# The second mixer's 24 feature chunks as pairs of seven block products, and its attention steps behind 14 gate chunks

## The chip, the core and the metric

The kernel runs on one core of a Trainium2 chip. The metric is the device time of one execution, in microseconds (us). Before the change three executions took 2940.22, 2941.33 and 2941.63 us, with a median of 2941.33 us. The profile was taken in an execution of its own.

## What is computed

The reference is one layer of a hybrid decoder on 512 prompt tokens and 8 sample tokens (N = 520 columns, kept as two halves of 260), all in float32. Cut to what matters here:

```python
sh1, sc1, g1, sh2, sc2, g2 = ada_mod(c, w_ada, b_ada)
h = modulate(rmsnorm(x, norm1_w), sh1, sc1)
mq, mk, mv, mo, mi, mf, fq, fk, fv, ff, ga, gb = jnp.split(h @ w_in + b_in, SPLIT_POINTS, axis=-1)
...                                       # the mLSTM mixer makes y_m
q_f = rmsnorm(split_heads(fq, F_HEADS), f_qnorm_w)
k_f = rmsnorm(split_heads(fk, F_HEADS), f_knorm_w)
y_f = fox_fn(q_f, k_f, v_f, lf_f)         # prompt: causal; sample: over pages of a cache
merged = jax.nn.sigmoid(ga) * (y_m @ w_proj_a) + jax.nn.sigmoid(gb) * (y_f @ w_proj_b)
x = x + g1 * (merged @ w_out)
...                                       # a gated feed-forward layer with a causal convolution
```

`h @ w_in` is the product that the change touches. Its columns are taken in chunks of 128 features: 1 chunk of forget and input gates, 24 of the mLSTM mixer, 24 of the second mixer (`fq`, `fk`, `fv` of 8 heads), 16 of `ga` and 16 of `gb`.

## The kernel before

**Two forms of the product.** A chunk of 128 features needs the 2048 inputs in 16 blocks of 128, times 520 columns. Every float32 operand is split into a high and a low part (`wh`, `wl` for weights, `hh`, `hl` for `h`), and three products of parts make one. `dense` (L206) does a chunk as it stands: 16 blocks, 3 products, 2 halves, 96 matmuls of 128x260, so 192 for two chunks. `Pair` (L255) does two chunks together as a 2 by 2 block product with seven block products instead of eight: 7 products of 8 blocks and 3 parts, 168 matmuls of 128x260. For it VectorE adds pieces of the raw weights (`total`, tiles `sw`), ScalarE and VectorE split seven blocks of weights, and the results in three accumulators `x`, `y` and `z` are put together by short additions (tiles `tt`, `tg`). `run_pairs` (L336) writes its instructions in a fixed order.

**Where the work around them stands.** `dense` calls `step` after each of the 16 blocks, and `step` takes the next entry of the list `bg`: a piece of an attention, or `None`. It also calls `due`, which now and then takes a step of `pending`, one of the 16 steps by which a slice of the `w_ada` product is made (two loads of 512 KB and four groups of matmuls, tile `adp`). A scheduler then orders the instructions of each engine, except inside `run_pairs`.

The stages that matter, with their times in the profile (from the span's start):

- 292 to 461 us, the mLSTM heads: dense chunks, with the mLSTM attention in `bg`.
- 461 to 574 us: `w_proj_a` (`pa`), dense, with `pending` making slice G1. Two dense gate chunks go before it (`NG` = 2).
- 574 to 736 us: 16 gate chunks (14 of `ga`, 2 of `gb`) in 8 units of `GatePair`. The forms of `h` that the seven products need (`hX`) are made during `pa`.
- 736 to 1084 us: the 24 chunks `fi` of the second mixer, dense, 3 for each head; slice SC2 in `pending`; the attention of a head in `bg` behind its chunks.
- 1084 to 1281 us: the other 14 chunks of `gb` (`gate`), dense; slice SH2 in `pending`; the attention of the sample tokens over the cache's pages in `bg`.
- 1281 to 1376 us: `w_proj_b` (`pb`), dense, and the merge.

**A head's attention** (L1141 to L1218): squares of q and k (`sq`, split into `hi` and `lo`; GpSimd makes `lo`), their sums by TensorE (`ms`), an inverse root by `rsqrt`, the split of q and k (`fqh`, `fql`, `fkh`, `fkl`; GpSimd makes the low parts), the spread of the forget row (`nFb`, copied to `nfb`), four blocks of scores (`fS`) with softmax (tiles `fs`, `sm`), their transposes (`fPT`), and the product with the values (`fy`).

**The sample's attention** (L1251 to L1336): GpSimd gathers 32 pieces of key pages (`kp`) and 32 of value pages (`vp`) by indirect DMAs. VectorE multiplies each `kp` with a broadcast query (`qb`) and sums it into `sc` (`s_scores`, kept in program order). A softmax follows (`sS`), its transposes (`sPT`), a memset of `pp` by GpSimd, and TensorE's products `sO` with `vp`, each four followed by a copy `ob` and transposes `sOT`.

Of the kernel before, what the change touches and what calls it, by code (L numbers as in the profile page):

```python
# [38 lines left out]
FQ, FK = 4, 7  # L39
FW = (2, 0, 0, 0, 4, 0)  # L40
# [25 lines left out]
def tile_hybrid_step(ctx: ExitStack, tc: tile.TileContext, I, O):  # L66
# [294 lines left out]
    def rsqrt(parts, scale, out=None):  # L361

        v, r, t = pt("rv"), out or st("rr"), pt("rt")
        for ps, a, b in parts:
            S.activation(r[:, a:b], ps, AF.Ln, scale=scale, bias=eps)
            V.tensor_scalar(v[:, a:b], ps, scale, EPS, op0=ALU.mult, op1=ALU.add)
# [599 lines left out]

    for hh in range(MH):
        H = Head()
        H.i, H.vt, H.hm, H.v, H.o = hh, [], [], [], []
        H.q = m_proj("q")  # L970
        H.k = m_proj("k")
        bg += [None, on(m_decay, H), on(m_rows, H), None, None, None]
        bg += [on(m_scores, H, j) for j in range(NB)] + [on(m_dots, H)]
        H.v = [m_proj("v"), m_proj("v")]
        bg += [None, on(m_values, H, 0), on(m_values, H, 1), on(m_states, H), None, on(m_den, H), None, on(m_bound, H),
               on(m_keys, H), None, None, None, on(m_num, H, 0), None, on(m_num, H, 1), None, on(m_state, H)]
        H.o = [m_proj("o"), m_proj("o")]
        bg += [None] * 12 + [on(m_tokens, H)] + [None] * 6 + [on(m_out, H)]
# [4 lines left out]
    def w_gate(j, which):  # L983
        i = 1 + 24 + 24 + which * KC + j
        acc = dense(I["w_in"][i], h, "gate")
        sg = st("sgm")
        S.activation(z2(sg), acc, AF.Sigmoid, bias=col(C_BIN + i - 1))
        return sg

    pending += ada_steps(G1)  # L990
    calls[1:] = 9, 10
# [29 lines left out]
    dsg = dram([NG, P, N], "dsg")  # L1021

    class GatePair(Pair):
        def __init__(self, gates, order):
            self.gates = gates
            super().__init__([I["w_in"][49 + g] for g in gates], hX, order, 1)
# [13 lines left out]
        def out(self, e):  # L1040

            g = self.gates[e]
            parts = (self.tt[:, :HN], self.tg[:, :HN]) if e == 0 else (self.tg[:, HN:N], self.tt[:, HN:N])
            for z, t in enumerate(parts):
                o = slice(z * HN, (z + 1) * HN)
                if g < KC:
                    V.tensor_tensor(t, t, self.pa[e][:, o], op=ALU.mult)
                G.dma_start((dmg[g] if g < KC else dsg[g - KC])[:, o], t)

        def after(self, r):  # L1050
            if r > 10:
                return
            b = [col(C_BIN + 48 + g) for g in self.gates]
            if r == 7:
                S.activation(self.tg[:, HN:N], self.x, AF.Sigmoid, bias=b[1], scale=-1.0)
                self.pa = []
                for g in self.gates:
                    self.pa.append(pt("pao") if g < KC else None)
                    if g < KC:
                        nc.sync.dma_start(self.pa[-1][:, :N], dmg[g])  # L1060
            if r == 8:
                S.activation(self.tt[:, HN:N], self.tt[:, HN:N], AF.Sigmoid, bias=b[1], scale=-1.0)
                S.activation(self.tt[:, :HN], self.tt[:, :HN], AF.Sigmoid, bias=b[0])
                S.activation(self.tg[:, :HN], self.tg[:, :HN], AF.Sigmoid, bias=b[0])
# [6 lines left out]
    gates = list(range(NG, KC + NG))  # L1071
    units = [GatePair(gates[2 * i:2 * i + 2], ORDER if i else ORDER1) for i in range(KC // 2)]
# [66 lines left out]
    yf = []  # L1139

    def f_norm(t, w, out):  # L1141
        r = rsqrt(sums_r(out.sq), 1.0 / DK)
        V.scalar_tensor_tensor(t[:, :N], t[:, :N], w, r[:, :N], op0=ALU.mult, op1=ALU.mult)

    def f_norm_k(H):
        f_norm(H.k, col(C_KN), H)
        G.dma_start(O["kT"][:, H.i, :], H.k[:, :N])
        V.tensor_copy(kS[:, :, H.i], H.k[:, SEQ:N])
        H.kr = split(sp, "s", H.k, "fk", SEQ, G)

    def f_norm_q(H):
        if H.i == 0:
            log_exp()
        f_norm(H.q, qwc, H)
        V.tensor_copy(qS[:, :, H.i], H.q[:, SEQ:N])
        H.qr = split(sp, "s", H.q, "fq", SEQ, G)

    def f_square(H, t):
        sq = pt("sq")
        S.activation(sq[:, :N], t[:, :N], AF.Square)  # L1160
        H.sq = parts_r(sq)

    def f_values(H):

        ps = mm_ps("vtp")
# [11 lines left out]
    def f_scores(H, i):  # L1177
# [13 lines left out]
        V.tensor_scalar(s[:, :n], s[:, :n], sm[:, 1:2], None, op0=ALU.mult)  # L1191
# [16 lines left out]
    def f_attend(H, j):  # L1208
# [8 lines left out]
        yf.append(split(sp, "s", H.y, "yf", SEQ))  # L1217
        H.vt = H.last = H.y = None  # L1218

    def f_proj(H, i):  # L1220
        acc, t, n = w_in("fi")
        S.activation(z2(t), acc, AF.Identity, bias=col(C_BIN + n - 1))
        return t

    pending += ada_steps(SC2)
    calls[:] = 0, 1, 3
    for hh in range(FH):
        H = Head()
        H.i, H.p, H.pt = hh, [], []
        H.q = f_proj(H, 0)  # L1230
        f_square(H, H.q)
        bg += [None] * FQ + [on(f_norm_q, H)]
        H.k = f_proj(H, 1)
        f_square(H, H.k)
        bg += [None] * FK + [on(f_norm_k, H)]
        H.v = f_proj(H, 2)
        G.dma_start(O["vT"][:, hh, :], H.v[:, :N])
        V.tensor_copy(vS[:, :, hh], H.v[:, SEQ:N])
        bg += [None] * FW[0] + [on(f_forget, H)] + [None] * FW[1] + [on(f_values, H)] + [None] * FW[2]
        for i in range(NB):  # L1240
            bg += [on(f_scores, H, i)] + [None] * FW[3]
        bg += [None] * FW[4] + [on(f_turn, H, j) for j in range(NB)] + [None] * FW[5]
        bg += [on(f_attend, H, j) for j in range(NB)]
# [7 lines left out]
    def s_rows():  # L1251
        ps = mm_ps("qSt")
        T.transpose(ps[:64, :P], qS.rearrange("p b h -> p (b h)"), ident)
        qrow = pt("qrow")
# [3 lines left out]
    def s_load(i):  # L1258

        b, e = divmod(i, 2)  # L1260
        qb = pt("qb")
        nc.sync.dma_start(qb[:, :512], dqf[b, e * 512:(e + 1) * 512].partition_broadcast(P))
        W.k[i] = [qb]
        for g in range(NPG):
            kp = pt("kp")
# [15 lines left out]
    def s_softmax():  # L1281
        pqk = pt("pqk")[:, :64]
# [25 lines left out]
    def s_gather(i):  # L1308

        e, g, b = i // 8 % 2, i // 4 % 2, i // 16 * 4 + i % 4  # L1310
        W.v[i] = pt("vp")
        gather(W.v[i][:, :512], I["cache_v"], idx_h[e][:, b * NPG + g:b * NPG + g + 1])

    def s_attend(n):
# [7 lines left out]
        if g == 1:  # L1322
            W.ob = pt("ob")
# [14 lines left out]
    bg += [s_rows] + [None] * 12 + [on(s_load, 0), None, None, on(s_load, 1)] + [None] * 5  # L1338
    for i in range(NS * 2):
        bg += [on(s_scores, i), None] + ([on(s_load, i + 2)] if i + 2 < NS * 2 else []) + [None] * 2  # L1340
    bg += [s_bias, None, s_softmax] + [None] * 6 + [s_weights] + [None] * 4
    bg += [on(s_gather, i) for i in range(6)] + [None] * 4
    for n in range(8):
        bg += [on(s_attend, n)] + [on(s_gather, i) for i in range(n * 4 + 6, min(n * 4 + 10, 32))]
        bg += [on(s_heads, n // 2)] if n % 2 else [None]
        bg += [None] * 3
    mg = []
    for j in range(KC):
        if j == 0:
            assert not pending  # L1350
            pending += ada_steps(SH2)
            calls[:] = 0, 1, 2
        if j < NG:
            mg.append(st("sgm"))
            nc.sync.dma_start(mg[j][:, :N], dsg[j])
        else:
            mg.append(w_gate(j, 1))
# [147 lines left out]
    early = {}  # L1505
    for n, j in enumerate(order):
# [15 lines left out]
        if n == KC - 1:  # L1522
            units[0].load((1, 0), (1, 1))
        old = pt("mgo")
# [624 lines left out]
```

## Time and profile before

| what | value |
|---|---|
| median of the runs | 2941.33 us |
| the profiled execution | 2941.65 us |
| its span, first to last instruction | 2940.0 us |
| TensorE's granted clock, mean | 0.997 |
| HBM read, written | 436.64 MB, 62.73 MB |
| stage of the 24 `fi` chunks | 348 us |
| stage of the 14 `gate` chunks | 197 us |

The span and the execution's own time differ by 1.65 us, which lie around the span. Busy times are sums by engine; "PE" is TensorE's matmuls, "PEld" its weight loads, DVE is VectorE, ACT ScalarE, POOL GpSimd, SP the engine that issues most loads. TensorE's matmuls are pipelined, so a matmul's duration (283 ns for 128x260) is longer than its distance to the next; the distance is read from a count of matmuls in a stretch without idle time.

### The profile page before, as it was taken

To read this page: it belongs to the slowest core of one execution; us is meant where nothing else is said; L and a number is where in the kernel's file an instruction comes from. 1 tells how busy PE (TensorE), PEld (TensorE's weight loads), DVE (VectorE), ACT (ScalarE), POOL (GpSimd) and SP (SyncE) were. 2 spreads that over 40 slices of the span, in tenths; PEclk is the share of its full clock that TensorE was granted. 3 is DMA by queue.
4 is the path that set the end of the run, shared out by engine and by line. 5 is a ranking of instruction groups with operands and counts; after the bars stand their busy time and mean duration, and the time that the engine had idled before them with its cause. 6 is when DMAs were issued, how large, how long until landed. Compare 5 with 4: busy or idle time off the path is not lost. (4 is left out here: it accounts for less than half of the span.)

```text
span 2940.0 us, 58499 instructions
## 1 busy us (share of the span) xinstructions
PE 2883.5 (98%) x23627; PEld 2750.5 (94%) x23627; DVE 2129.8 (72%) x3866; ACT 1292.4 (44%) x2182; POOL 424.1 (14%) x662
## 2 busy tenths in 40 slices
PE   6999999999999999999999999999999999999999
PEld 4888998899999999899999999999999999999999
DVE  4777875578455556248888888888888887788787
ACT  4234433355444442234555444444444455544543
POOL 0003431201111114411211100000000001100100
PEclk9999999999999999999999999999999999999999
DMA  9833437945444348767673343444444436745843
GB/s 339 285 108 112 146 123 261 293 146 166 137 133 143 120 165 298 256 207 223 199 239 111 101 151 126 147 140 149 133 138 140 144 122 183 190 155 190 205 159 109
DMA packets 209592, 506.67 MB, mean 172 GB/s; under 512 B 22624, under 2 KB 75216, under 8 KB 209320
## 3 DMA queue, kind: packets, MB, share of 16 engines
q1 hardware_dynamic: 174000, 412.24, 42.9%
q0 software_dynamic: 34880, 90.45, 10.2%
q8 instruction: 185, 3.03, 0.4%
q14 instruction: 87, 0.71, 0.1%
q10 hardware_dynamic: 440, 0.23, 0.0%
HBM read 436.64 MB, written 62.73 MB: 170 GB/s over the span
## 5 line engine op out<-in xcount | busy, mean ns | idle before, releaser
L62 PE MATMUL x<-bf,wh 128*128 128x260 f32 x2624 | 476.8, 283 | 1.0 <-DVE tg L62 0.5
L62 ACT CAST wh<-sw 128x512 fp32r<-128x512 f32 x584 | 334.9, 621 | 244.4 <-PE z L62 86.9
L62 DVE TENSOR_TENSOR wl<-sw,wh 128x512 fp32r<-128x512 f32 x584 | 375.9, 685 | 69.7 <-ACT wh L62 66.8
L62 PEld LDWEIGHTS x<-bf,wh 128*128 128x128 f32 x2624 | 403.6, 188 | 1.4 <-DVE tg L62 0.7
L180 DVE TENSOR_TENSOR wl<-raw,wh 128x1024 fp32r<-128x1024 f32 (+1 forms) x168 | 208.6, 1243 | 265.9 <-ACT wh L179 249.9
L62 DVE TENSOR_TENSOR wl<-raw,wh 128x1024 fp32r<-128x1024 f32 (+2 forms) x283 | 310.6, 1105 | 118.5 <-ACT wh L62 114.5
L62 ACT CAST wh<-raw 128x1024 fp32r<-128x1024 f32 (+2 forms) x283 | 268.1, 956 | 234.3 <-PE x L62 128.9
L62 PE MATMUL x<-bf,wl 128*128 128x260 f32 x1312 | 369.6, 282 | 0.0
L179 ACT CAST wh<-raw 128x1024 fp32r<-128x1024 f32 (+1 forms) x168 | 173.4, 1033 | 354.3 <-PE gate L222 68.5
L62 PEld LDWEIGHTS x<-bf,wl 128*128 128x128 f32 x1312 | 247.0, 188 | 0.0
L62 PE MATMUL y<-bf,wh 128*128 128x260 f32 x1312 | 240.6, 284 | 2.9 <-ACT wh L62 2.4
L62 PEld LDWEIGHTS y<-bf,wh 128*128 128x128 f32 x1312 | 202.7, 189 | 3.4 <-ACT wh L62 2.6
L62 PE MATMUL x<-ff,wh 128*128 128x260 f32 x1024 | 186.3, 282 | 0.0
L62 PE MATMUL y<-bf,wl 128*128 128x260 f32 x656 | 185.8, 283 | 0.2 <-DVE wl L62 0.2
L62 DVE TENSOR_TENSOR sw<-raw,raw 128x512 f32<-128x512 f32 x288 | 185.0, 683 | 0.4 <-DMA tot<-sq 0.4
L222 PE MATMUL fi<-hh,wh 128*128 128x260 f32 x768 | 162.3, 293 | 0.0
L62 PEld LDWEIGHTS x<-ff,wh 128*128 128x128 f32 x1024 | 157.9, 188 | 0.0
L222 PE MATMUL fi<-hl,wh 128*128 128x260 f32 x768 | 155.0, 283 | 0.0
L222 PE MATMUL fi<-hh,wl 128*128 128x260 f32 x768 | 154.1, 282 | 0.0
L62 PE MATMUL x<-ff,wl 128*128 128x260 f32 x512 | 144.7, 283 | 0.0
L222 PEld LDWEIGHTS fi<-hh,wh 128*128 128x128 f32 x768 | 118.5, 189 | 15.9 <-ACT wh L179 6.7
L62 PE MATMUL fo<-fe,wh 128*128 128x260 f32 x768 | 125.7, 284 | 1.9 <-DVE fo L62 1.1
(585 smaller groups left out, 7448.6 us busy)
## 6 DMA issues: line engine op xcount, KB each, us to landing
raw<-in_w_fi SPq DMA_DIRECT2D x176, 512.0 KB, 4.5
raw<-in_w_in SPq DMA_DIRECT2D x156, 512.0 KB, 4.8
ar<-in_w_ada SPq DMA_DIRECT2D x192, 256.0 KB, 6.0
raw<-in_w_ada SPq DMA_DIRECT2D x96, 512.0 KB, 4.0
raw<-in_w_fo SPq DMA_DIRECT2D x64, 512.0 KB, 4.1
raw<-in_w_out SPq DMA_DIRECT2D x32, 512.0 KB, 4.7
raw<-in_w_fo SPq DMA_DIRECT2D x32, 384.0 KB, 4.3
dff<-cc POOLq DMA_DIRECT2D x44, 260.0 KB, 4.0
```

The lines of the kernel that those rows point to most:

```text
L62: return lambda *a, **k: self.tc.keep_in_program_order(getattr(self.eng, op)(*a, **k))
L179: S.copy(wh[:, o], t[:, :m])
L180: V.tensor_tensor(wl[:, o], t[:, :m], wh[:, o].bitcast(F32), op=ALU.subtract)
L222: T.matmul(acc[:, z, :HN], a[:, o], b[:, z * HN:(z + 1) * HN], start=(k == 0 and i == 0), stop=(k == K - 1 and i == 2))
```

## The change

The 24 chunks `fi` leave the dense form and join the gate chunks in `MixPair`: 12 units for the second mixer ahead of the 8 units of gates, 20 units in one run. A unit's features are written to a DRAM tensor `dfi` and read back by `f_load`, a head at a time. The 24 dense chunks behind which the attention stood are gone, so all of the second mixer's attention, the prompt's and the sample's, stands behind the 14 dense `gate` chunks, in 14 x 16 = 224 slots, by a table of times (`plan`, `at`).

Three sets of steps move: slice G1 of `w_ada` goes from the `pa` stage to the mLSTM heads, SC2 from the `fi` stage to the two gate chunks and `pa`, and SH2 stays. In the attention, the scaling of the softmax and one of `rsqrt`'s two first steps go from VectorE to ScalarE. The sample's tiles move to the larger pool. The output of heads 0 to 3 is written to DRAM (`dyf`) and read back late (`f_again`). The dense gate chunks are stored without the sigmoid (`dsg`), read back in the `pb` stage (`mg_load`), and the sigmoid is taken there.

```diff
-    def rsqrt(parts, scale, out=None):
+    def rsqrt(parts, scale, out=None, act=False):
...
+            if act:
+                S.activation(v[:, a:b], ps, AF.Identity, scale=scale, bias=eps)
+            else:
+                V.tensor_scalar(v[:, a:b], ps, scale, EPS, op0=ALU.mult, op1=ALU.add)
...
+    pending += ada_steps(G1)
+    calls[:] = 0, 3, 5
     for hh in range(MH):
...
-    pending += ada_steps(G1)
-    calls[1:] = 9, 10
+    pending += ada_steps(SC2)
+    calls[:] = 0, 9, 10
...
-    class GatePair(Pair):
+    class MixPair(Pair):
...
-                G.dma_start((dmg[g] if g < KC else dsg[g - KC])[:, o], t)
+                G.dma_start((dfi[i] if g < 0 else dmg[g] if g < KC else dsg[g - KC])[:, o], t)
...
+    chunks = [*range(NFI), *range(NFI + NG, NFI + KC + NG)]
+    units = [MixPair(chunks[i:i + 2], ORDER if i else ORDER1) for i in range(0, len(chunks), 2)]
...
-        V.tensor_scalar(s[:, :n], s[:, :n], sm[:, 1:2], None, op0=ALU.mult)
+        S.activation(s[:, :n], s[:, :n], AF.Identity, scale=sm[:, 1:2])
...
-        acc, t, n = w_in("fi")
...
+    plan = [[] for _ in range((KC - NG) * KC)]
...
+    starts = [S0 + 18 * h for h in range(5)] + [S0 + 72 + 22 * h for h in range(1, 5)]
...
+        for j in range(NB):
+            at(t + 2 * j, f_scores, H, j)
+            at(t + 10 + j, f_turn, H, j)
+            at(t + 14 + j, f_attend, H, j)
...
+    for i in range(NS * 2):
+        at(t + 9 + 5 * i, s_scores, i)
...
+    for n in range(8):
+        at(t + 9 + 4 * n, s_attend, n)
+        for i in range(4 * n + 8, min(4 * n + 12, 32)):
+            at(t + 9 + 4 * n, s_gather, i)
...
+    pending += ada_steps(SH2)
+    calls[:] = 0, 1, 2
+    for j in range(NG, KC):
+        t = w_gate(j, 1)
+        G.dma_start(dsg[j], t[:, :N])
...
+        if j >= NG:
+            S.activation(mg[j][:, :N], mg[j][:, :N], AF.Sigmoid)
```

**Place 1, TensorE, the first feature chunk.** Before, a dense chunk `fi`: each of the three products of a block runs over both halves (x2), and 16 blocks make 96 matmuls.

```order
L222 MATMUL fi_8598<-hh_331,wh_8601 128x260 x2
L222 MATMUL fi_8598<-hl_332,wh_8601 128x260 x2
L222 MATMUL fi_8598<-hh_331,wl_8602 128x260 x2
L222 MATMUL fi_8598<-hh_338,wh_8601 128x260 x2
L222 MATMUL fi_8598<-hl_339,wh_8601 128x260 x2
```

Now, the second unit of pairs (`x` is one of the unit's accumulators):

```order
L61 MATMUL x_6917<-hh_331,wh_6872 128x260
L61 MATMUL x_6917<-hl_332,wh_6872 128x260
L61 MATMUL x_6917<-hh_331,wl_6873 128x260
L61 MATMUL x_6917<-hh_338,wh_6872 128x260
L61 MATMUL x_6917<-hl_339,wh_6872 128x260
```

Each block product takes one half of the columns. Over the whole program TensorE's matmuls go from 23000 to 22712: 2304 of `fi` are gone, and there are 1152 more of `x`, 576 more of `y` and 288 more of `z`.

**Place 2, VectorE, the last block of scores of a middle head.** Before, between the row maximum (`ISA fs`) and the reciprocal of the row sum stand a weight split `wl` and rows of the same softmax:

```order
L1187 ISA fs_11171,sm_11172<-fS_11166,nfb_11089 128x512
L1187 ISA sm_11172 128x1
L180 TENSOR_TENSOR wl_11279<-raw_11276,wh_11278 128x1024
L1190 RECIPROCAL sm_11154<-sm_11154 128x1
L1188 TENSOR_SCALAR sm_11172<-sm_11172 128x1
L1191 TENSOR_SCALAR fs_11153<-fs_11153,sm_11154 128x384
L1190 RECIPROCAL sm_11172<-sm_11172 128x1
L1191 TENSOR_SCALAR fs_11171<-fs_11171,sm_11172 128x512
```

Now, head 5's, with the key pages between:

```order
L1202 ISA fs_13797,sm_13798<-fS_13792,nfb_13473 128x512
L1202 ISA sm_13798 128x1
L1190 COPY nfb_13812<-nFb_13810 128x512
L1203 TENSOR_SCALAR sm_13798<-sm_13798 128x1
L61 TENSOR_TENSOR kp_13648<-kp_13648,qb_13646 128x512
L233 TENSOR_TENSOR fvl_13858<-vtp_13852,fvh_13857 128x384
L61 TENSOR_REDUCE sc<-kp_13648 128x4
L1205 RECIPROCAL sm_13798<-sm_13798 128x1
```

The multiply and the sum of a key page, and the next head's `nfb` and `fvl`, now stand inside a head's softmax, and the scaling of `fs` has left VectorE. From the fifth `nfb` row to the last sum into `sc`, 197 rows stand on VectorE: 64 of key pages, 11 weight splits `wl`, 122 of heads. In the same piece TensorE has 619 matmuls of `gate` (from the fifth `nFb` to `sS`).

**Place 3, TensorE, the value pages.** Before, four `sO` and then nine blocks of a `gate` chunk until the next four (three rows of which are shown):

```order
L1320 MATMUL sO_14174<-vp_14034,pp_12616 32x512
L1320 MATMUL sO_14174<-vp_14042,pp_12616 32x512
L1320 MATMUL sO_14174<-vp_14100,pp_12616 32x512
L1320 MATMUL sO_14174<-vp_14108,pp_12616 32x512
L222 MATMUL gate_14149<-hh_512,wh_14152 128x260 x2
L222 MATMUL gate_14149<-hl_513,wh_14152 128x260 x2
L222 MATMUL gate_14149<-hh_512,wl_14153 128x260 x2
```

Now, near the end of the last `gate` chunk:

```order
L1330 MATMUL sOT_15047<-ident,ob_15015 128x128 x4
L1319 MATMUL sO_15068<-vp_14979,pp_11780 32x512
L1319 MATMUL sO_15068<-vp_14981,pp_11780 32x512
L1319 MATMUL sO_15068<-vp_14983,pp_11780 32x512
L221 MATMUL gate_15028<-hh_1560,wh_15113 128x260
L221 MATMUL gate_15028<-hl_1561,wh_15113 128x260 x2
L221 MATMUL gate_15028<-hh_1560,wl_15114 128x260 x2
L221 MATMUL gate_15028<-hh_1567,wh_15113 128x260
L1319 MATMUL sO_15068<-vp_14985,pp_11780 32x512
```

From the transposes `sPT` to the last `sO` there were 456 matmuls of `gate`, and now there are 152; 12 of `adp` and 12 of `sOT` stand there too. On POOL's queue the memset of `pp`, which waits for `sPT`, has 24 of the 32 value gathers behind it, before and now.

More of the change, by code (lines that the diff above doesn't have):

```diff
@@ L38 @@
 G_WAIT = 8
[L39 to L40 removed]
+NFI = 3 * 8
 C_ADA = 0
@@ L1505, in tile_hybrid_step @@
     early = {}
+    for j in order[:2]:
+        mg_load(j)
     for n, j in enumerate(order):
```

188 lines of the change are left out of this document (105 added, 83 removed).

## The prediction

> **What bounds the kernel now.** I began with the page: busy times by engine and the slices.
>
> ```profile
> PE 2883.5 (98%) x23627; PEld 2750.5 (94%) x23627; DVE 2129.8 (72%) x3866; ACT 1292.4 (44%) x2182; POOL 424.1 (14%) x662
> ...
> PEclk9999999999999999999999999999999999999999
> ```
>
> TensorE (PE) is busy for 98% of the span with its clock granted throughout, so what counts is its number of matmuls and each idle gap. The windows by stage come next. Columns: the window, its length, busy time of PE, PEld, DVE, ACT and POOL, granted clock, share of the DMA engines, GB/s.
>
> ```profile
> 292.00:461.00 169.00, 165.88 (x1269) 155.26 (x1272) 127.88 (x220) 72.33 (x114) 56.53 (x59) 1.00 0.45 146
> ...
> 736.00:1084.00 348.00, 348.00 (x2796) 324.71 (x2796) 180.31 (x371) 147.64 (x263) 52.34 (x51) 1.00 0.41 136
> 1084.00:1281.00 197.00, 196.54 (x1586) 173.33 (x1585) 88.28 (x154) 50.77 (x75) 72.15 (x66) 1.00 0.76 264
> 1281.00:1376.00 95.00, 95.00 (x788) 93.00 (x787) 70.97 (x121) 35.66 (x55) 8.17 (x16) 1.00 0.57 186
> ```
>
> In the two stages that the change rebuilds, 736 to 1281 us, PE loses 0.46 us in all, while VectorE is busy for about half. The waits of PE there have one row (engine, line, what it waited for; total, times, longest):
>
> ```profile
> PE gate L222 <- DVE wl L180: 0.5, 1, 0.5
> ```
>
> So nothing can be won there except by fewer matmuls, and a new wait is paid in full. What a matmul costs comes from stretches without idle time: one of `w_proj_b` (no attention beside it), and the busiest of the gate stage.
>
> ```profile
> 1310.00:1370.00 60.00, 60.00 (x500) 60.00 (x500) 48.06 (x82) 24.59 (x39) 5.27 (x10) 1.00 0.57 183
> 1115.00:1190.00 75.00, 74.54 (x609) 68.19 (x608) 56.88 (x80) 16.18 (x19) 40.35 (x35) 1.00 0.92 324
> ```
>
> 500 matmuls of 128x260 in 60 us make 0.120 us each.
>
> **Term 1, fewer matmuls.** 24 dense chunks are 24 x 96 = 2304 matmuls; 12 paired units are 12 x 168 = 2016. 288 x 0.120 = **34.6 us saved**. The rest of the old stage doesn't vanish: 348 - 2304 x 0.120 = 71.5 us is other work of PE. Of it the `w_ada` slice (tile `adp`, same columns without DVE and POOL) is
>
> ```profile
> 736.00:1084.00 348.00, 17.05 (x128) 2.52 (x128) 0.58 (x1) 1.00 0.41 136
> ```
>
> 17.05 us, which moves to the two gate chunks and `pa`; the slice that stood in `pa` moves to the mLSTM heads. These are the same matmuls at another place: 0. The other 54.5 us are the heads' attention, some 7.2 us a head for the seven and a half that fit in the stage. They move into the gate stage, which becomes 197 + 54.5 = 251 us long (224 slots of 1.12 us).
>
> Sentences on the Trainium skill, which the sum does without: its page "TensorE: Matmul & The Clock Gate", section "Wait — 56ns, not 53.3ns?", gives the distance of matmuls as columns over 2.4 GHz and some 2.5 ns, by which 260 columns are an estimated 110.8 ns and the saving 31.9 us. The trace's 120 ns, taken with these operands, decides.
>
> **Term 2, the tail of the value pages.** After the last softmax, POOL clears `pp` once PE has made `sPT`, and behind that memset stand 24 of the 32 value gathers, in order. From the timeline of POOL before (start, length, what it is, idle before it):
>
> ```profile
> 1195.07 0.53 POOL L1301 MEMSET pp<- 128x512 f32 x1 [4.62 <-PE sPT L1299]
> ...
> 1252.31 0.95 POOL L651 DMA_INDIRECT vp<-in_cache_v,idx  x1 [0.30 <-PE gate L222]
> 1253.56 1.80 POOL L651 DMA_INDIRECT vp<-in_cache_v,idx  x1 [0.30 <-issue]
> 1255.66 0.94 POOL L651 DMA_INDIRECT vp<-in_cache_v,idx  x1 [0.30 <-issue]
> 1256.91 0.95 POOL L651 DMA_INDIRECT vp<-in_cache_v,idx  x1 [0.30 <-issue]
> ```
>
> A gather follows the one before after 1.25 us, and now and then one takes 0.9 us more. Before, POOL waited in this part for PE; now PE has fewer matmuls between. Groups of PE in 1195 to 1275 us (busy, mean ns), and the landing time in the view of tile `vp`:
>
> ```profile
> L1320 PE MATMUL sO<-vp,pp 128*32 128x512 f32 x64 | 8.5, 605 | 0.0
> L420 PE MATMUL adp<-raw,cs 128*32 128x512 f32 x48 | 6.4, 605 | 0.0
> L1331 PE MATMUL sOT<-ident,ob 128*128 128x128 f32 x16 | 2.5, 276 | 0.0
> ...
> DMA to landing us min/median/max: 3.3/4.2/7.7
> ```
>
> By the order, PE's work from `sPT` to the last `sO` is now 152 gate matmuls (18.2 us), all the `sO` (8.5), 12 of 16 `sOT` (1.9) and half of these `adp` (3.2): 31.8 us, where 456 gate matmuls alone were 54.7. POOL needs 0.5 for the memset, 24 x 1.25 = 30 for the gathers, 0.9 for one long gather, 1 for a store of `dsg` in its queue, and 4.2 to the last landing, which also counts the issue (0.95): 35.7 to 36.6. PE thus waits some 4 to 5 us, and a little more since `sO` comes in fours and the last gathers release it one by one. With the least landing it is 3.5, with the largest 9. **I take +6.**
>
> **Term 3, VectorE in the middle.** From the fifth head's `nfb` to the last sum into `sc` the order has 197 rows of DVE: 64 of key pages, 11 of `wl`, 122 of heads. Groups of DVE, 736 to 1281 us (count, busy, mean ns, idle time before and what ended it):
>
> ```profile
> L180 DVE TENSOR_TENSOR wl<-raw,wh 128x1024 fp32r<-128x1024 f32 x76 | 94.9, 1249 | 167.2 <-ACT wh L179 155.2 <-PE ms L397 11.9
> L62 DVE TENSOR_REDUCE sc<-kp 128x4 f32<-128x512 f32 x32 | 22.0, 686 | 1.1
> L62 DVE TENSOR_TENSOR kp<-kp,qb 128x512 f32<-128x512 f32 x32 | 21.9, 684 | 1.8 <-DMA kp<-in_cache_k,idx 1.6
> ...
> L1187 DVE CUSTOM_DVE_ANT_0 fs<-fS,nfb 128x128 f32<-128x128 f32 (+3 forms) x32 | 15.7, 491 | 9.5 <-PE fS L1184 9.5
> ...
> L234 DVE TENSOR_TENSOR fpl<-fPT,fph 128x512 fp32r<-128x512 f32 (+2 forms) x24 | 13.4, 558 | 14.8 <-ACT fph L233 14.8
> L1191 DVE TENSOR_SCALAR fs<-fs,sm 128x128 f32<-128x128 f32 (+3 forms) x32 | 12.4, 386 | 0.3
> L366 DVE TENSOR_SCALAR rv<-ms 128x260 f32<-128x260 f32 x32 | 12.1, 420 | 3.0 <-ACT rr L365 3.0
> ...
> L234 DVE TENSOR_TENSOR yfl<-fy,yfh 128x512 fp32r<-128x512 f32 x8 | 5.5, 692 | 30.0 <-ACT yfh L233 30.0
> ...
> L1190 DVE RECIPROCAL sm<-sm 128x1 f32<-128x1 f32 x32 | 5.1, 160 | 8.3 <-ACT fs L1189 8.3
> ...
> L234 DVE TENSOR_TENSOR fvl<-vtp,fvh 128x384 fp32r<-128x384 f32 x8 | 4.5, 557 | 9.4 <-ACT fvh L233 9.4
> ```
>
> Key pages take 43.9 us and 11 `wl` 13.7. DVE is busy for 180.31 + 88.28 = 268.6 us in both stages; without 94.9, 43.9, and the 12.4 and 12.1 that go to ScalarE (42% and 26% busy in the two stages, room for it) 105.3 us stay for eight heads, 13.2 us or 35 rows each, 0.376 us a row. 122 rows are 46 us. Together **DVE needs 103.6 us**. PE in the same stretch has 619 gate matmuls (74.3 us), 32 records of `adp` (4.3) and 3.7 heads (27): **105.6 us**. The two are equal, and DVE is only so quick if it never waits. Its waits for ACT or PE inside a head were, in the rows above, 9.5 + 14.8 + 30.0 + 8.3 + 9.4 = 72 us, 9.0 a head, free of charge while DVE had half its time spare. The weights are split up to two half chunks ahead of PE (11.5 us), and key pages can fill gaps, so part is absorbed. Lower bound 0 (everything filled), upper bound 3.7 x 9 = 33 less the 2 spare, 31. The nearest row is 1115 to 1190 us: DVE busy at 76% with all 43.9 us of key pages in it, and PE lost 0.46. Here it is 98% over 105 us. **I take +6**, one fifth of the upper end.
>
> **Term 4, smaller things.** The mLSTM heads take slice G1's 128 `adp` beside 76% of DVE, where PE already waits; the largest of its rows:
>
> ```profile
> PE qkn L826 <- DVE dt L799: 2.4, 3, 0.8
> ```
>
> `adp` occupies there one of the buffers in which attention results stand; once more these waits would be 3. The `pa` stage keeps its slice count, and `pb` loads gates and takes 14 sigmoids on an ACT that is busy for 35.66 of 95 us: 0 as long as a load lands within a chunk of 96 x 0.120 = 11.5 us. I take **+1.5** (0 to 4). The kernel's DMA rate in the crowded part stays near the 324 GB/s of the row above, at which PE ran on: 0; that cover would be gone if gathers landed at 7.7 instead of 4.2 us, which is the upper end of term 2.
>
> **Sum.** -34.6 + 6 + 6 + 1.5 = -21.1. The profiled execution is 2941.65 us (span 2940.0 and 1.65 around it), 0.3 over the runs' median: 2941.65 - 21.1 = **2920.6**, on the runs 2920.
>
> **The rivals.**
>
> *No stall: 2907.* The order's slack and the waits of PE's own chain absorb terms 2 to 4 (2941.65 - 34.6). For it: 0.46 us lost in 545 us so far. Against it: POOL's 36 us behind the memset don't fit into 32.
>
> *DVE bounds the middle: 2932.* Half of the 33 us of waits are exposed: 103.6 + 16.5 - 105.6 = 14.5, with terms 2 and 4 at 6 and 1.5 and nothing else, 2907 + 22 = 2929; with all of them, 31, it is 2945.5, no change to speak of. I put the rival at 2932, nearer to the half. For it: the ten rows above. Against it: in 1115 to 1190 us nothing of the kind reached PE.
>
> *POOL holds up the heads: slower, 2966.* GpSimd works in order, and the key gathers now stand between the small parts (`lo`, `fkl`, `fql`) of heads 5 to 7, 12 rows. Groups and waits of POOL, 736 to 1281 us:
>
> ```profile
> L651 POOL DMA_INDIRECT kp<-in_cache_k,idx x32 | 36.6, 1145 | 54.2 <-DVE sc L62 29.3 <-DMA dqf<-qrow 18.5 <-issue 6.1
> ...
> L389 POOL TENSOR_TENSOR lo<-sq,hi 128x520 fp32r<-128x520 f32 x16 | 20.9, 1307 | 138.8 <-DVE hi L388 138.8
> ...
> POOL kp L651 <- DVE sc L62: 29.3, 10, 7.7
> ```
>
> Four gathers of 1.145 + 0.3 and a wait for a free `kp` of 29.3 / 10 = 2.9 make up to 8.7 us ahead of such a row. The plan leaves four or five slots, 5.0 us, between squares and their sums, less `hi` and `lo` themselves (0.4 and 1.3): a cushion of 3.3. Slower begins where the 12 waits are on the mean 26.6 / 12 = 2.2 us over the cushion, 5.5; at the full 8.7 all 12 cost 65 and the time is 2985; the middle is 2966. Against it: a row seldom meets all four gathers and the wait.
>
> On the same pairing, and needed for no number here: the Trainium skill's page "SBUF — State Buffer", section "Who interferes with whom", says that a VectorE instruction with two inputs in SBUF (`kp` times `qb`) and a GpSimd instruction that reads SBUF (`lo`, `fkl`, `fql`) block one another for a whole instruction. This speaks against the change, in this rival's direction; before, these stood in different stages, and no row shows them together.
>
> *The pairing gains nothing* can't be: 288 matmuls are gone from an order that is never waiting.
>
> **How the numbers follow.** The forecast, 2913 to 2928, has 0.43; no stall 0.18; DVE 2928 to 2940 has 0.22, of which a third lies within 0.2% (2935.5 to 2947.2), about what a measurement of this kernel can tell from no change; other sums in that band 0.07; POOL, slower, 0.10. So faster 0.43 + 0.18 + 0.15 = 0.76 and some of the ends, 0.77; same 0.13; slower 0.10. The range takes in no stall below, with 2 us for a shorter matmul distance, and terms 2, 3 and 4 at 9, 20 and 4 above: 2905 to 2940.
>
> **What would show it.** Right: PE matmuls down by 288, a stretch of 12 units in 242 us with no idle, a gate stage near 265 us, PE waits for `vp` near its end of about 6 us, and waits for `wl`, `fs` or `fpl` in its second half of about as much. No stall: PE idle under 1 us there. DVE: busy at 95% or more over 100 us, and PE waiting for `wl`. POOL: PE waiting for `ms` or `fS` with `lo`, `fkl` or `fql` behind. Wrong in term 1 if the units run slower than 0.120 us a matmul, as in a first unit that waits for the inputs' forms.

## The result, and the profile after

The changed kernel takes 2992.64 us (median of 4 runs, 2991.26 to 2993.69), the kernel before 2941.48 us on the same chip: a ratio of 1.0176, 95% interval 1.0163 to 1.0188. It is **slower by 51 us** (1.8%) where 21 us less were forecast. The profiled execution took 2992.55 us. First its page: the span, the busy times and TensorE's granted clock in 40 slices.

```profile
span 2990.9 us, 58746 instructions
...
PE 2891.3 (97%) x23339; PEld 2730.7 (91%) x23339; DVE 2232.4 (75%) x4054; ACT 1378.8 (46%) x2438; POOL 465.3 (16%) x740
...
PEclk9999999999999998989999999999999999999999
```

The 288 matmuls are gone from PE's count, and yet PE is busy for 8 us more, and two slices of the clock show an 8. The windows by stage say where: the 20 paired units; the gate stage up to its last 52 us; those 52 us; and the stage of `w_proj_b`.

```profile
594.00:998.00 404.00, 402.50 (x3356) 401.91 (x3355) 311.66 (x527) 210.05 (x418) 50.44 (x92) 1.00 0.46 151
999.00:1280.00 281.00, 250.40 (x1763) 212.72 (x1766) 181.31 (x376) 141.53 (x306) 113.96 (x119) 0.94 0.64 210
1280.00:1332.00 52.00, 41.02 (x194) 20.13 (x187) 4.70 (x24) 6.48 (x14) 23.07 (x24) 0.84 0.66 235
1332.00:1427.00 95.00, 93.47 (x781) 92.28 (x780) 70.30 (x125) 44.32 (x72) 7.81 (x15) 1.00 0.67 217
```

The pairs came as forecast: 20 x 168 x 0.120 = 403, and they took 404.6, with three waits of 0.5 to 0.6 us at their start. `w_proj_b` is as it was. The gate stage, from the end of the pairs at 998.2 to the first `pb` at 1331.8, is 333.6 us long where its work is 251: **82 us are lost in it**. 41.6 of them are idle time of PE. A granted clock of 0.94 over 281 us and of 0.84 over 52 lacks 17 and 8 us of full speed, 25 in all. Some 15 us are in neither, and the section on the tail comes back to them. The five largest waits of PE in the stage (what was waited for: total, times, longest):

```profile
PE adp L422 <- DMA raw<-in_w_ada: 13.5, 5, 4.7
PE ms L399 <- POOL lo L391: 10.0, 5, 5.3
PE gate L221 <- issue: 4.0, 4, 1.8
PE ms L399 <- DVE sm L1202: 3.7, 2, 1.9
PE fPT L1216 <- DVE sm L1202: 2.8, 1, 2.8
```

Before, 545 us had one such wait of 0.5. The mLSTM stage is the other place. By the first `gate` matmul (view of tile `gate`, before and then after; duration in ns, min/median/max, then first and last start in us) it ends 25.3 us later, of which 17 are the slice G1 that moved in:

```profile
L222 PE MATMUL gate<-hh,wh x512: 277/282/391, 433.7 to 1280.4; 128*128 128x260 f32 x171
```

```profile
L221 PE MATMUL gate<-hh,wh x512: 277/282/587, 459.0 to 1330.7; 128*128 128x260 f32 x171
```

The two gates and `w_proj_a` behind them give 3.7 back (138.1 to 134.4 us). The sum: -34.6 + 82 + 8.3 - 3.7 = +52, and the span grew by 50.9.

### The profile page after: what moved, and what is told of

It is laid out like the page before. It is cut to its first block, busy times and chain, and to the rows that moved or that the text cites. A ratio compares the mean times of both kernels' runs of the same rounds, so it can differ in the third digit from the quotient of the medians.

```text
span 2990.9 us, 58746 instructions
## 1 busy us (share of the span) xinstructions
PE 2891.3 (97%) x23339; PEld 2730.7 (91%) x23339; DVE 2232.4 (75%) x4054; ACT 1378.8 (46%) x2438; POOL 465.3 (16%) x740
## 3 DMA queue, kind: packets, MB, share of 16 engines
q0 software_dynamic: 40608, 104.77, 11.5%
## 5 line engine op out<-in xcount | busy, mean ns | idle before, releaser
L61 DVE TENSOR_TENSOR wl<-sw,wh 128x512 fp32r<-128x512 f32 x680 | 438.8, 688 | 91.4 <-ACT wh L61 88.5
L61 ACT CAST wh<-sw 128x512 fp32r<-128x512 f32 x680 | 389.8, 621 | 244.8 <-PE z L61 87.9
L61 DVE TENSOR_TENSOR wl<-raw,wh 128x1024 fp32r<-128x1024 f32 (+2 forms) x355 | 359.3, 1027 | 122.3 <-ACT wh L61 114.4
L61 ACT CAST wh<-raw 128x1024 fp32r<-128x1024 f32 (+2 forms) x355 | 309.6, 889 | 290.6 <-PE x L61 147.5
L179 DVE TENSOR_TENSOR wl<-raw,wh 128x1024 fp32r<-128x1024 f32 (+2 forms) x120 | 150.1, 1252 | 141.8 <-ACT wh L178 132.7
L178 ACT CAST wh<-raw 128x1024 fp32r<-128x1024 f32 (+2 forms) x120 | 123.2, 1028 | 242.3 <-DMA raw<-in_w_in 33.3
L61 DVE TENSOR_TENSOR sw<-raw,raw 128x512 f32<-128x512 f32 x336 | 216.3, 686 | 0.3 <-DMA tot<-sq 0.3
L61 PE MATMUL x<-hf,wh 128*128 128x260 f32 x960 | 175.4, 283 | 1.0 <-ACT wh L61 0.6
L61 PEld LDWEIGHTS x<-hf,wh 128*128 128x128 f32 x960 | 147.9, 188 | 1.4 <-ACT wh L61 0.7
L61 PE MATMUL x<-hf,wl 128*128 128x260 f32 x480 | 135.5, 282 | 0.0
L61 PEld LDWEIGHTS y<-bf,wl 128*128 128x128 f32 x656 | 124.1, 189 | 0.4 <-DVE wl L61 0.4
```

The costliest lines, as they stand in the source:

```text
L61: return lambda *a, **k: self.tc.keep_in_program_order(getattr(self.eng, op)(*a, **k))
L178: S.copy(wh[:, o], t[:, :m])
L179: V.tensor_tensor(wl[:, o], t[:, :m], wh[:, o].bitcast(F32), op=ALU.subtract)
```

## The experiments

Each run is compared with the kernel before on its own chip (the changed kernel: +51.2), whose times were 2940.6 to 2944.8 us. "Loss" is the length of the stage from the last pair to the first `pb`, less its work: 251 us, and 11.5 for each dense feature chunk in it (12 less in e1 and e3, 17 more in c6 and c7, by what was moved out or in; of c8's and c9's loss 3 us are SC2's first matmuls). The changed kernel ran 4 times, c8 4 and c9 6 times, and each other run once. Single executions of one kernel lay up to 9 us apart (c9: 2927.1 to 2935.6), and the unchanged stage of k1 lost 76 us instead of 82, so differences of some 6 us or less between single runs are not read as effects.

| run | time | against before | loss in the stage |
|---|---|---|---|
| changed kernel | 2992.6 | +51.2 | 82 |
| e1, SH2 late | 2998.0 | +53.3 | 81 |
| e2, low parts on DVE | 2982.8 | +38.0 | 72 |
| e3, no pages | 2932.9 | -11.9 | 31 |
| e4, early memset | 2994.5 | +53.1 | 79 |
| k1, delays | 3047.3 | +102.6 | 76 |
| h6, six dense | 2949.3 | +8.0 | 27 |
| h12, twelve dense | 2983.2 | +41.8 | 56 |
| h12b, twelve, tables | 2944.9 | +2.9 | 16 |
| c2, six, low parts, memset | 2943.1 | +1.8 | 24 |
| c3b, twelve, low parts, memset | 2942.6 | +0.7 | 12 |
| t3, changed, four value pages | 2965.7 | +22.4 | 53 |
| t2, c2 with four value pages | 2928.6 | -12.0 | 12 |
| c6, c2 with G1 and SC2 back | 2948.0 | +6.0 | 35 |
| c7, ten, G1 and SC2 back | 2945.0 | +3.0 | 23 |
| c8, six, slices spread | 2953.4 | +12.7 | 40 |
| c9, ten, slices spread | 2932.8 | **-7.9** | 12 |

### What a wait of PE costs (k1)

```diff
+    dl = mconst([P, 512], "dl")
+    G.memset(dl[:, :512], 0.0)
...
+    def delay(n):
+        ps = mm_ps("dl")
+        T.matmul(ps[:, :P], ident, ident, start=True, stop=True)
+        S.copy(dl[:, :P], ps[:, :P])
+        for _ in range(n):
+            G.tensor_tensor(dl[:, :512], dl[:, :512], dl[:, :512], op=ALU.subtract)
+        T.matmul(ps[:, :P], ident, dl[:, :P], start=True, stop=True)
-    run_pairs(units, 1, {}, 0)
+    run_pairs(units, 1, {14 * i + 17: (lambda n=n: delay(n)) for i, n in enumerate((1, 3) * 4)}, 0)
```

> Eight artificial waits in the stretch of 20 paired units, where PE had no idle time: PE waits for one GpSimd subtraction (about 2 us) in four places and for three in a row (about 4.7 us) in the four others, 28 us apart by turns. Plain theory: the time grows by the idle time alone, some 27 us, to 3019. Clock theory: PE's granted clock falls behind a long wait, so that each of the four long ones costs about twice its idle time and the short ones only theirs: 3035 to 3045, with rows of PEclk under 1.00 behind the long waits only.

(The delays came 47 us apart.) The wait row is 34.6 us for 8 waits, and the stretch of pairs went from 404.6 to 459.1 us, 54.5 more. The 16 small matmuls are 3 us at most; **some 17 us, 2 us for each wait, are slowed clock**. (The granted clock of the stretch, 0.96 on the mean over 459 us, agrees: some 18 us.) It shows in the timeline of PE (start, length, what, idle before): behind 3.03 us of waiting the matmuls follow at 0.215 us instead of 0.12, for 3.6 us.

```profile
651.87 0.49 PE L61 MATMUL dl<-dl,ident 128*128 128x128 f32 x2 [3.03 <-POOL dl L1126]
652.11 0.41 PE L61 MATMUL y<-hh,wh 128*128 128x260 f32 x1
652.31 0.42 PE L61 MATMUL y<-hl,wh 128*128 128x260 f32 x1
652.53 0.42 PE L61 MATMUL y<-hh,wl 128*128 128x260 f32 x1
...
655.75 0.28 PE L61 MATMUL y<-hh,wl 128*128 128x260 f32 x1
655.87 0.28 PE L61 MATMUL y<-hh,wh 128*128 128x260 f32 x1
```

The clock theory holds, but for its bound: the four short waits (3.0 to 3.8 us) cost too. The Trainium skill, page "TensorE: Matmul & The Clock Gate", section "HAM oscillation — how this bites in real kernels", warns of idle gaps of PE above some 3.4 us, after which the clock is halved. The trace agrees in the halved rate and not in the bound: here a gap of 3.0 us does it.

### What stands behind the waits (e1 to e4)

```diff
     (e1)
-    pending += ada_steps(SH2)
-    calls[:] = 0, 1, 2
+    calls[:] = 0, 1, 1
     for j in range(NG, KC):
+        if j == KC - 1:
+            pending += ada_steps(SH2)
```

> Slice SH2 of the w_ada product starts in the last gate chunk and is made beside w_proj_b; nothing else changes. Theory (the adp steps wait for raw weights in the crowded stage): the 13.5 us that PE waited for in_w_ada go, and as much again of slowed clock behind those waits, so the time falls from 2992 to about 2966, with w_proj_b longer by the 17 us of adp and the gate stage shorter by about 44. Rival (the raw buffers come late because DVE is late, whoever asks for them): PE waits for wl or raw of the gate chunks instead, and the time stays at 2985 to 2992.

The rival came true in its main point: with all `adp` gone from the stage but for its last chunk, the waits for `raw` are gone, others stand in their place, and nothing is won. They aren't the ones that it named, `wl` or `raw` of the gate chunks, but these (the largest waits of PE in the stage of e1):

```profile
PE gate L221 <- ACT sgm L991: 13.1, 3, 10.5
PE ms L399 <- POOL lo L391: 8.5, 7, 2.9
PE sO L1319 <- DVE pp L1302: 4.8, 1, 4.8
```

The longest, 10.5 us, can be followed back. VectorE came to the first key page before the page had landed and waited 6.17 us; the next head's `fk` stood behind it in its order; ScalarE waited for `fk`, with the end of a gate chunk (`sgm`) behind it; and PE waited for the accumulator that `sgm` frees:

```profile
1151.81 0.69 DVE L61 TENSOR_TENSOR kp<-kp,qb 128x512 f32<-128x512 f32 x1 [6.17 <-DMA kp<-in_cache_k,idx]
1156.28 0.76 DVE L1165 SCALAR_TENSOR_TENSOR fk<-fk,sv,rr 128x520 f32<-128x520 f32 x1
1157.07 0.62 ACT L232 CAST fkh<-fk 128x512 fp32r<-128x512 f32 x1 [9.66 <-DVE fk L1165]
1157.60 0.69 ACT L991 ACTIVATE sgm<-gate,sv 128x520 f32<-128x520 f32 x1
1158.34 0.59 PE L221 MATMUL gate<-hh,wh 128*128 128x260 f32 x1 [10.50 <-ACT sgm L991]
```

In the changed kernel VectorE waits at the same place, with a weight split `wl` behind the page:

```profile
1154.90 0.69 DVE L61 TENSOR_TENSOR kp<-kp,qb 128x512 f32<-128x512 f32 x1 [7.35 <-DMA kp<-in_cache_k,idx]
1155.63 0.69 DVE L61 TENSOR_REDUCE sc<-kp 128x4 f32<-128x512 f32 x1
1156.23 1.22 DVE L179 TENSOR_TENSOR wl<-raw,wh 128x1024 fp32r<-128x1024 f32 x1
```

There two waits of `adp` for raw tiles stand close together. The second (2.25 us, to 1160.99) is for a load that was issued at 1157.5, after this `wl`. The first (4.49 us, to 1156.82) is not VectorE's: its load was issued at 1151.8, behind a step of `adp` that freed the tile, and was simply landing. The row of PE names the last link (a raw tile, an accumulator), and another link is last as soon as that one is removed.

```diff
     (e2)
-        H.sq[x] = parts_r(sq)
+        H.sq[x] = parts_r(sq, V)
...
-            H.kr = split(sp, "s", H.k, "fk", SEQ, G)
+            H.kr = split(sp, "s", H.k, "fk", SEQ, V)
...
-        H.qr = split(sp, "s", H.q, "fq", SEQ, G)
+        H.qr = split(sp, "s", H.q, "fq", SEQ, V)
```

> The low parts lo, fkl and fql of the eight heads are made by VectorE instead of GpSimd (32 rows of some 0.7 us more on DVE). Theory (GpSimd's order: the low parts stand behind key gathers): the 10.7 us that PE waited for lo and fql go, with as much of slowed clock, so about 2971. Rival (DVE bounds the stage, as one of the prediction's rivals had it): 22 us more of DVE make it slower, 2995 to 3015.

More work on VectorE made the kernel 13 us faster (+38.0 instead of +51.2). The waits for `lo` are gone; those for `raw` of `in_w_ada` rise from 13.5 to 19.1. So GpSimd's order is a cause, and VectorE's load isn't. In the changed kernel's own timelines, `hi`, which `lo` needs, is made by 1205.9, and three gathers in GpSimd's order go before `lo`, behind one under way:

```profile
1205.46 0.42 DVE L390 CAST hi<-sq 128x520 fp32r<-128x520 f32 x1
...
1206.63 1.54 POOL L653 DMA_INDIRECT kp<-in_cache_k,idx  x1 [0.30 <-issue]
1208.48 1.31 POOL L653 DMA_INDIRECT kp<-in_cache_k,idx  x1 [0.30 <-issue]
1210.09 1.23 POOL L653 DMA_INDIRECT kp<-in_cache_k,idx  x1 [0.30 <-issue]
1211.34 1.30 POOL L391 TENSOR_TENSOR lo<-sq,hi 128x520 fp32r<-128x520 f32 x1
```

The matmul that needs it, at 1212.69, had waited 5.31 us.

```diff
     (e4)
+        W.z = st("pz")
+        G.memset(W.z[:, :512], 0.0)
         pqk = st("pqk")[:, :64]
...
-        G.memset(pp[:, :512], 0.0)
-        pz = pp[:, :512].rearrange("p (g b i) -> p g b i", g=NPG, b=NS)
+        pz = W.z[:, :512].rearrange("p (g b i) -> p g b i", g=NPG, b=NS)
```

> The zeroes under the sample's weights stand in a tile of their own and are written before the softmax, so that no memset on GpSimd waits for PE with value gathers behind it. Theory of the prediction's second term (the value gathers behind the memset hold up the tail): the tail from 1280 to 1332 us, 33 us of PE's work in 52, shortens by 10 to 19, to 2973 to 2983. Rival (the tail waits for something else: raw weights of the w_ada slice, or instructions): within 3 us of 2992.

+53.1: nothing gained. The memset is not what holds up the tail. (In the changed kernel GpSimd comes to it at 1276.7 and doesn't wait for `sPT`.)

In e3 the list of attention steps ends with the heads (`s_rows` to `s_heads` aren't called, and `yS` is zero).

> The sample's page attention is left out whole (its gathers, scores, softmax and products; its output is zero), the heads stay where they are. It is 13 us of PE's work. Theory (page attention and heads collide on the in-order queues): the stage falls from 333 to about 250, the time to about 2910. Rival (the heads alone, at 18 slots each, are too tight, with adp between them): most gaps stay, and the time is 2950 to 2965. Where PE's gaps in 1000 to 1140 us stay as they are, before the first key page, they belong to the heads.

Neither: 63 us less than the changed kernel against its own before, between the two forecasts. 12 of them are PE's work on the pages, so page attention costs 51 us beyond its work, and the heads alone still lose 31. The gaps in 1000 to 1140 us stayed as they were.

### Spreading the attention out (h6, h12, c2)

```diff
     (six; with twelve: 12, and calls 0, 1, 3)
-    chunks = [*range(NFI), *range(NFI + NG, NFI + KC + NG)]
+    ND = 6
+    chunks = [*range(NFI - ND), *range(NFI + NG, NFI + KC + NG)]
...
-    plan = [[] for _ in range((KC - NG) * KC)]
+    plan = [[] for _ in range((KC - NG + ND) * KC)]
...
-        plan[t].append(on(f, *a))
+        plan[t * (KC - NG + ND) // (KC - NG)].append(on(f, *a))
...
-    calls[:] = 0, 1, 2
+    calls[:] = 0, 2, 5
+    for i in sorted(range(NFI - ND, NFI), key=lambda i: (i % 3 > 0, i)):
+        acc = dense(I["w_in"][25 + i], h, "fi")
+        t = st("fi")
+        S.activation(z2(t), acc, AF.Identity, bias=col(C_BIN + 24 + i))
+        G.dma_start(dfi[i], t[:, :N])
```

> The last 6 feature chunks (heads 6 and 7) go back to the dense form ahead of the gate chunks, and the plan of the attention is stretched over 20 dense chunks instead of 14, all else as changed. That gives back 6 x 12 = 72 matmuls (8.6 us) of the 34.6. Theory (the attention stands too thickly behind its matmuls: of the 82 us that the stage lost, most come from chains of several engines that have two or three slots to get ready): the loss falls by more than half, so 2992 + 9 - 45 = 2955 or less. Rival (fixed losses, from queues in order and from transfers, whatever the spacing): the loss stays, 2992 + 9 = 3001.

> As before, with 12 feature chunks (heads 4 to 7) dense, so 26 dense chunks behind which the attention is stretched; 144 matmuls (17.3 us) of the saving are given back. Theory (density): the loss is down to some 10 us, about 2992 + 17 - 72 = 2937. Rival (fixed losses): 3009.

Six dense chunks cost 8.6 us of matmuls and win 43 in all; the loss falls from 82 to 27. That is density, of the attention's steps and of the `adp` steps between them, which the same edit spaces out (two calls in five instead of one in two). With twelve the kernel was slower again, and the groups of ScalarE in that run say why (busy, mean ns):

```profile
L364 ACT ACT_TABLE_LOAD x22 | 28.2, 1283 | 0.3
...
L370 ACT ACT_TABLE_LOAD x18 | 23.1, 1283 | 0.3
```

In the changed kernel each of these rows has 4, and the program has 23 loads of tables instead of 60. By the order of ScalarE's instructions, the one load that keeps logarithm and exponential in one table now stood ahead of another table's load. With a load of that table put behind the pairs:

> The run with twelve dense feature chunks again, with ScalarE's table for log and exp loaded once behind the pairs (in that run the table was loaded 36 times more, 1.28 us each, while PE waited for ACT). Theory (density): what is left of the loss is some 10 us, 2935 to 2942. If it stays over 2960, the table loads were not what made the run with twelve slower than the one with six.

+2.9, loss 16. Density goes on paying: 82, 27, 16 us lost with 14, 20 and 26 dense chunks.

> Six dense feature chunks as in the run with six, the low parts of the heads on VectorE, and the early memset, all three together. If the losses add up (density more than half, order on GpSimd 13, memset some): 2935 to 2945. If they are the same loss seen three times, no better than the run with six dense chunks alone, within 4 us.

> Twelve dense feature chunks, the table loaded once, the low parts of the heads on VectorE and the early memset. If density and GpSimd's order are the causes, nearly nothing of the loss in the crowded stage remains but the tail: 2928 to 2938. If the rest of the loss lies elsewhere (the mLSTM stage with slice G1, the tail), no better than the run with twelve and tables, within 3 us.

c2 is 6 us better than h6 (+1.8), at most: less than the 13 that the low parts won alone, so partly the same loss seen twice. c3b, +0.7, can't be told from h12b. In c2 the windows show the middle clean and the loss at the end: 1.7 us idle in 260, then 7.5 in 82.

```profile
940.00:1200.00 260.00, 258.28 (x1969) 230.12 (x1962) 188.71 (x400) 146.16 (x309) 61.01 (x77) 1.00 0.68 229
```

```profile
1200.00:1282.00 82.00, 74.53 (x568) 61.12 (x567) 18.01 (x47) 17.44 (x30) 37.46 (x43) 0.94 0.73 240
```

VectorE, busy for 181 of 281 us in the changed kernel, is busy for 189 of 260 here, a larger share, and PE hardly waits.

### The tail (t2, t3)

```diff
     def s_gather(i):
...
-        W.v[i] = st("vp")
-        gather(W.v[i][:, :512], I["cache_v"], idx_h[e][:, b * NPG + g:b * NPG + g + 1])
+        if i < 4:
+            W.vc[i] = st("vp")
+            gather(W.vc[i][:, :512], I["cache_v"], idx_h[e][:, b * NPG + g:b * NPG + g + 1])
+        W.v[i] = W.vc[i % 4]
```

> The run with six dense chunks, low parts on VectorE and early memset, with only the first 4 of the 32 value pages gathered and used eight times each (the sample's rows of the output are other numbers, all matmuls stay). In the tail of that run PE lost some 8 us in waits that the profile gives no releaser for (issue), and slowed clock behind them, while gathers ran back to back. If the gathers' traffic holds up PE's instructions, those waits go and the time falls from 2943 to 2930 or below; if they come from PE's own mix of sO and gate matmuls, they stay and the time is 2940 or more.

> The changed kernel itself with only the first 4 of the 32 value pages gathered and used eight times each (the sample's rows of the output are other numbers, all matmuls stay, the memset too). This prices the second term of the prediction, the tail, inside the changed kernel: its tail holds 33 us of PE's work in 52. If the gathers are all that is wrong there, the time falls by 15 to 20, to 2973 to 2978; if the wait for a raw w_ada tile at the start of the tail (4.7 us, and slowed clock) belongs to the weights and not to the gathers, by 8 to 12 only, and the wait stays in the row of adp.

Both fell further than expected: t2 by 14 us against c2, t3 by 29 against the changed kernel. In t2 the same 82 us (the last 12 of them already in `w_proj_b`) have no idle time and the full clock:

```profile
1200.00:1282.00 82.00, 82.00 (x666) 70.91 (x665) 23.34 (x59) 22.79 (x36) 8.69 (x15) 1.00 0.56 183
```

The whole stage of t2 has 1.8 us of waits and a clock of 1.00, and yet a "loss" of 12. So some 10 us of each loss are not waiting: the sum that gives 251 us puts the work too low by about as much, and most of the 15 us that were in neither row in the changed kernel are of this kind. Why that work takes longer isn't shown.

So the value gathers do make the tail, and not by their place behind the memset. Whether their traffic does it or their 1.25 us each in GpSimd's order, these two runs don't part; that PE waits only 0.3 us for `vp` itself, and otherwise for a raw tile's DMA or for nothing named, speaks for the traffic. In the timeline of PE in the changed kernel, `adp` first waits for a raw tile, and later matmuls whose operands are there wait for nothing that the profile names:

```profile
1285.48 1.07 PE L422 MATMUL adp<-raw,cs 128*32 128x512 f32 x2 [4.73 <-DMA raw<-in_w_ada]
...
1308.93 0.28 PE L221 MATMUL gate<-hl,wh 128*128 128x260 f32 x1 [1.02 <-issue]
1310.35 1.03 PE L1319 MATMUL sO<-vp,pp 128*32 128x512 f32 x2 [1.13 <-issue]
1313.17 0.61 PE L221 MATMUL gate<-hh,wl 128*128 128x260 f32 x2 [1.78 <-issue]
```

In the tails of t2 and t3 both kinds are gone. The waits called issue look like instructions that come late. The Trainium skill, page "Runtime: NRT & Kernel Launch", section "Instruction fetch mechanics", has each engine fetch its code by a DMA queue of its own and calls the cost mostly hidden. The trace agrees: its DMA records have a queue of kind instruction with 183 transfers of 16 KB, one for each 256 or so of PE's instructions. Three of them lie between 1250 and 1330 us, at 1258.0, 1273.1 and 1298.9, and took 1.0 to 1.1 us, the median of all being 0.97. None is under way during the waits above. So late code doesn't explain them, and what does stays open.

### The place of the slices (c6 to c9)

c6 and c7 put G1 back beside `w_proj_a` and SC2 before SH2 in the dense stage. c8 and c9 put G1 back, keep SH2, and start SC2 in the last gate chunk, so that it is made beside `w_proj_b`. All have the low parts on VectorE, the early memset and the table load.

> Six dense feature chunks, low parts on VectorE, early memset, and in addition the slices of w_ada where they stood before the change: G1 beside w_proj_a, SC2 and SH2 beside the dense chunks of the second mixer and the gates. If moving G1 to the mLSTM heads cost the 4 us that stage lost beyond its 17 us of work, the time falls by about 4 against 2943. If the slices are free wherever they stand, it is 2943; if 16 more adp steps among the heads crowd them (the density theory), it is slower, 2945 to 2960.

> Ten dense feature chunks, otherwise as the run with six and the slices of w_ada put back. 120 matmuls (14.4 us) of the saving of 34.6 are given back. Density theory: the loss in the crowded stage is 5 us and the tail's some 10, so 2941 - 20 + 15 = 2936; if SC2 among the heads crowds them, 2940 or more.

The mLSTM stage is whole again (first `gate` at 431.5 and 431.1), so term 4's place is confirmed, but with SC2 back in it the crowded stage loses more than the mLSTM stage gives back (35 us with six dense chunks, where c2 lost 24; +6.0 and +3.0 in all).

> Six dense feature chunks, low parts on VectorE, early memset, with the slices of w_ada spread: G1 beside w_proj_a as before the change, SH2 behind the dense chunks, SC2 beside w_proj_b. If the mLSTM stage lost some 8 us by slice G1 and w_proj_b can take a slice at the price of its 17 us of matmuls alone, 2943 - 8 + 3 (w_proj_a's own waits come back) = 2938, faster than both kernels by 3 us. If w_proj_b is lengthened by more than the 17, 2942 or more.

> The same with ten dense feature chunks: 4 x 12 = 48 matmuls (5.8 us) more. If the crowded stage still loses something to density with six, which ten would save (the run with twelve lost some 8 us there, the run with six 17), the time is 3 us under that of six; if the tail is what is left, whatever the density, it is 6 us over it.

c9 is **faster than both kernels**: 2932.76 us, ratio to before 0.9968, 95% interval 0.9955 to 0.9980. It has two calls of `adp` in five besides the ten chunks, which its expectation doesn't say. Its stage of 378 us:

```profile
877.00:1255.00 378.00, 375.61 (x2956) 336.52 (x2954) 218.50 (x458) 178.62 (x355) 98.89 (x124) 1.00 0.70 232
```

c8 lost 40 us in the stage at c2's density, with waits of 8.7 for `hi` and 5.5 for raw tiles. Its `adp` steps come at every second call instead of two in five, and its instructions stand in another order. Which of the two did it wasn't tried, so c9 against c8 doesn't price the four more dense chunks alone.

## Why the prediction was wrong

**Term 1 was right.** 288 matmuls fewer, and 404.6 us for 20 units where the forecast's 0.120 us a matmul makes 403. The sum of the rest was wrong.

**"A new wait is paid in full" failed first.** It is paid more than once: k1 shows some 2 us of slowed clock behind a wait of 3 to 6. In the gate stage 41.6 us of idle time stand beside 25 of slowed clock, and no term of the sum held that. The two stages that were rebuilt could not show it before, since PE never paused there, but other places of the same trace could. Behind a wait of 1.86 us PE worked at half the clock for 3.41 us (the timeline of PE, then the window with the columns of the prediction's):

```profile
203.08 0.51 PE L606 MATMUL pre<-hh,wh 128*128 128x260 f32 x2 [1.86 <-DVE pre L613]
```

```profile
203.74:207.15 3.41, 3.41 (x18) 3.41 (x18) 2.76 (x6) 2.05 (x4) 0.00 (x0) 0.50 0.00 0
```

Two more pauses, of 1.83 us to 268.5 and 2.39 us to 1628.7, were followed by the same, and that trace's pauses of 1.1 to 1.6 us weren't. The length alone doesn't decide: a pause of 2.77 us in the changed kernel, to 1230.3, left the clock at 1.00, and the same pause of 2.75 us in t3 came with 6.8 us at 0.50.

**Term 3 (+6) was the failed step in size: some 53 us.** It weighed VectorE's durations against PE's and took a fifth of the waits inside a head. VectorE never was the bound (65% busy; e2 gave it more and won 13). What cost time was chains through four in-order engines with two or three slots to get ready, where one late link (`lo` behind gathers, a key page not yet landed) stops all behind it; e1's chain of four engines and the runs with more dense chunks show that. The 53 us hold the slowed clock and most of the 10 us that are not waits. 31 us of it belong to the heads alone (e3) and 22 to the key pages (51 in e3, less 29 in t3), if the parts add up. The comparison with 1115 to 1190 us, where key pages cost nothing, was misleading: no head ran beside them there.

**Term 2 (+6) was 29** (t3). The direction was right, the reason wrong: the memset costs nothing (e4), and PE hardly waits for `vp` (0.3 us), but the gathers cost it time all the same. The sentence that DMA adds 0 because PE had run on at 324 GB/s did not hold: the mean rate in the tail was lower (235 GB/s), and a rate at which PE ran on once is no cover for what loads and gathers do elsewhere.

**Term 4 (+1.5) was 8.3, and 4.6 with what `w_proj_a` gave back.** The place was right (c6).

**The rivals.** "DVE bounds the middle" is out. "POOL holds up the heads", given 0.10 at 2966, named a mechanism that was there (10 us of waits, 13 by e2) but a sixth of the loss. That it had the direction right was mostly luck. The blocking of GpSimd by VectorE that the prediction mentions beside it doesn't show: `lo` took 1.31 us in the median, as before. The range had its upper end at 2940 because each mechanism was priced alone and as if only its own rows could wait.

What stays open: why single matmuls wait beside gathers; what makes the 10 us that are neither idle time nor slowed clock; how much of a change of 10 us in these runs comes from the new order of instructions rather than from what was moved (e1 and c8).

## What to carry to other kernels

Fewer matmuls in a kernel that is bound by them win only what the work hidden behind them still finds room for: count not only the busy time of the other engines, but the slots between the steps of each chain, and give some of the saving back if the chains get tight (the fast version keeps ten dense chunks, 14.4 of 34.6 us, and its slices apart). Price a wait of TensorE of 2 us or more at its idle time and about 2 us more. A wait's row names the last link; before removing it, look at which engine's head of line it shares with the others.

## What the runs showed of the hardware

A pause of TensorE of 3.0 us brings matmuls at 0.215 us instead of 0.12 for the next 3.6 us (k1), and one of 1.86 us can bring half the clock for 3.41 us (the kernel before). With value gathers back to back, single matmuls waited up to 1.8 us with no releaser, which went away with the gathers, and no transfer of code was under way then. And a load of ScalarE's table (1.283 us) that moves in the order can multiply: 35 more of them came with 39 us (h12 against h12b).
